# A causal mask read as 3 KB runs on 128 partitions, with a shuffle matrix in the band matmul, in a batched matmul and softmax

## Chip, cores, metric

One core of one Trainium2 chip. The metric is the device time of one execution in microseconds (us). A run is compared with runs of the kernel before on the same chip in the same job.

## The reference

```python
# x: 16 x 512 x 512, weight: 512 x 512, mask: 512 x 512 (1 strictly below the diagonal)
y = scale * np.matmul(x, weight)          # scale = 0.125
y = np.where(mask == 1, y, -1e9)
y_exp = np.exp(y - np.max(y, axis=-1, keepdims=True))
return (y_exp / np.sum(y_exp, axis=-1, keepdims=True)).astype(np.float32)
```

Row 0 is fully masked, so it comes out as 1/512 everywhere. Traffic that no version avoids is x (16.8 MB in) and the result (16.8 MB out).

## The kernel before

Work goes in 16 units u of 512 rows. Two units are a group of 2 MB: half h of the rows of four batches. For h = 0 only the left 256 columns are computed. A partition holds eight consecutive rows (slots t). One unit is: a cast of x to bf16 on VectorE (DVE), 16 transposes on TensorE (PE) into PSUM (PE's result memory), two copies back (DVE and ScalarE, called ACT), and then for each of the four slots four matmuls with the weight, one matmul that adds the mask's band (the 256 columns of this half in which the diagonal lies), the exponential on ACT with its row sum, and the division on DVE.

```python
load(0, slots(0))                       # first half of x group 0, 1 MB
for b in range(KT):                     # four diagonal 128x128 blocks of the mask
    seq(nc.sync.dma_start(diag_f32[b * DP : (b + 1) * DP],
        mask[r : r + P, r : r + P].rearrange("(p t) c -> p t c", t=S)))
seq(nc.sync.dma_start(w_f32, ...))      # weight, 1 MB
load(0, slots(1))
for g in range(1, X_BUFS): load(g)      # groups 1 to 4 of x, 2 MB each
...
spin(12)                                # filler matmuls on zeros: PE busy until data comes
...
cast(0); transpose(0); evict(0)
# diag_f32 -> 0 / -512 -> four matmuls that repeat rows -> eight copies -> band
...
for u in range(U + 1):
    if u + 1 < U: transpose(u + 1)
    if u + 2 < U: cast(u + 2)
    if u + 1 < U: evict(u + 1)
    if u < U:     multiply(u)
    if u >= 1:    normalise(u - 1); ...store, and load of group g + 5
```

Every transfer is issued by the SyncE queue (SP), in program order. Each is split over the same 16 DMA engines.

The softmax here doesn't subtract the row's maximum and nothing guards it: scores larger than these inputs give would overflow.

## Time and profile before

| | before |
|---|---|
| median time | 90.65 us (90.54 to 90.81) |
| span of the profiled run | 89.0 us |
| PE busy | 81% |
| DMA engines, data | 94% of 16 engines' span |
| moved | 34.95 MB |
| last store issued / last landing / end | 82.43 / 88.21 / 89.04 us |

Read it in this order: which resources are busy throughout, then which of them has work waiting in front of it. The prediction below does this with the lines. One part of the page that it doesn't show is that of the DMA issues (what, issuer, count, KB each, us from issue to landing):

```profile
xf<-in_x_dram SPq DMA_DIRECT2D x7, 2048.0 KB, 17.0
out_dram<-ot SPq DMA_DIRECT2D x6, 2048.0 KB, 13.8
diag_f<-in_mask_dram SPq DMA_DIRECT2D x4, 64.0 KB, 4.9
```

A transfer of 2 MB needs 4.9 us of engine time (the prediction's steps between landings) and lands 13.8 to 17 us after its issue: most of that it waits behind other transfers, so the DMA queue has work in front of it.

### The profile page before, as it was taken

The numbers are of one execution on the slowest core, as the hardware profiler recorded it, in microseconds if no ns is written. First come the engines' busy times: TensorE is split into PE (matmuls) and PEld (weight loads), VectorE is DVE, ScalarE is ACT, GpSimd is POOL, SyncE is SP. The second block draws the span as 40 slices with busy tenths as digits, with TensorE's granted clock in tenths as the row PEclk, the third lists the DMA queues.
The fourth block names the chain that finished last, engine by engine and source line by source line (L and its number), as shares of the span: only waits on it lengthen the run. The fifth ranks groups of instructions, "written<-read, shape, count | busy, mean of one in ns | idle before, by whom it ended". The sixth has DMA issues, their size and how long they took to land.

```text
span 89.0 us, 1583 instructions
## 1 busy us (share of the span) xinstructions
PE 72.1 (81%) x585; PEld 49.6 (56%) x592; DVE 61.0 (68%) x121; ACT 55.9 (63%) x154; POOL 6.6 (7%) x14
## 2 busy tenths in 40 slices
PE   4994503999999999999999999999999999980000
PEld 1324103878955659995565999556599965530000
DVE  4856785079994877999687699977689880528000
ACT  5300593445977868698687779768777977671000
POOL 7940000000200000020000002000000200000000
PEclk9999855558999999999999999999999999999555
DMA  0998999999999999999998999999999999999770
GB/s 11 390 228 328 420 464 434 405 449 420 427 434 405 434 394 427 467 427 375 456 442 383 471 427 383 464 434 397 449 427 405 449 420 420 456 401 420 324 320 15
DMA packets 3462, 34.95 MB, mean 392 GB/s; under 512 B 384, under 2 KB 896, under 8 KB 896
## 3 DMA queue, kind: packets, MB, share of 16 engines
q1 hardware_dynamic: 3456, 34.87, 94.0%
q8 instruction: 4, 0.07, 0.3%
q14 instruction: 2, 0.02, 0.0%
HBM read 18.09 MB, written 16.78 MB: 392 GB/s over the span
## 4 chain that ended last, share of the span: by engine, by line
PE 73%; DMA 10%; SPq 4%; DVE 3%; issue 1%; ACT 1%; DVEq 0%; ACTq 0%
PE py L122 48%; PE pt L98 16%; DMA xf<-in_x_dram 10%; PE py L131 8%; SPq L174 3%; DVE ot L158 1%; DVE xb L89 1%; SPq L85 1%; ACT ot L141 1%; SPq L179 1%; DVEq L290 0%; DVE rinv L156 0%; ACTq L290 0%
## 5 line engine op out<-in xcount | busy, mean ns | idle before, releaser
L122 PE MATMUL py<-w_bf,xt 128*128 128x256 bf16 (+1 forms) x249 | 51.0, 334 | 0.4
L141 ACT ACTIVATE ot<-py 128x256 f32<-128x256 f32 (+1 forms) x64 | 31.2, 493 | 8.9 <-PE py L131 8.8
L122 PEld LDWEIGHTS <-xt 128*128 128x128 bf16 x256 | 25.3, 101 | 12.8
L109 ACT COPY xt<-pt 128x1024 bf16<-128x1024 bf16 x16 | 16.2, 1012 | 12.8 <-PE pt L98 8.0
L89 DVE CAST xb<-xf 128x2048 bf16<-128x2048 f32 x16 | 19.5, 1221 | 5.8 <-DMA xf<-in_x_dram 5.8
L158 DVE TENSOR_SCALAR ot<-ot,rinv 128x256 f32<-128x256 f32 (+1 forms) x64 | 23.0, 423 | 0.7
L98 PE MATMUL pt<-ident_bf,xb 128*128 128x128 bf16 x256 | 17.8, 225 | 5.1 <-DVE xb L89 5.1
L98 PEld LDWEIGHTS <-xb 128*128 128x128 bf16 x256 | 16.6, 116 | 7.5 <-DVE xb L89 6.7
L131 PE MATMUL py<-band,ident_bf 128*128 128x256 bf16 x64 | 17.9, 280 | 0.0
L108 DVE COPY xt<-pt 128x1024 bf16<-128x1024 bf16 x16 | 11.0, 688 | 7.8 <-PE pt L98 7.8
L141 ACT ACTIVATION_READ_ACCUMULATOR ot<-py 128x1 f32 x64 | 12.8, 201 | 0.0
L131 PEld LDWEIGHTS <-ident_bf 128*128 128x128 bf16 x64 | 6.5, 101 | 4.3
L160 POOL MEMSET ot<- 4x256 f32 x4 | 1.8, 448 | 63.1 <-DVE ot L158 63.1
L190 PE MATMUL py<-zeros 128*128 128x512 bf16 x12 | 5.3, 632 | 1.2 <-DVE zeros L185 1.2
L156 DVE RECIPROCAL rinv<-rsum 128x4 f32<-128x4 f32 x16 | 2.7, 168 | 5.1 <-ACT ot L141 5.1
L198 DVE MEMSET ot<- 128x2048 f32 x2 | 3.5, 1765 | 0.8 <-issue 0.8
L190 PEld LDWEIGHTS <-zeros 128*128 128x128 bf16 x12 | 1.6, 144 | 3.9 <-issue 2.8
L233 ACT CAST band<-py 64x512 bf16<-64x512 f32 x4 | 2.3, 580 | 1.1 <-DVE band L233 1.0
L233 DVE CAST band<-py 64x512 bf16<-64x512 f32 x4 | 2.5, 675 | 0.5 <-PE py L222 0.5
L222 PE MATMUL py<-diag_bf,spread 64*128 64x512 bf16 x4 | 1.2, 412 | 0.9 <-DVE diag_bf L209 0.9
L196 POOL MEMSET band<- 64x2048 bf16 x1 | 1.8, 1800 | 0.1
L195 POOL MEMSET band<- 64x2048 bf16 x1 | 1.8, 1802 | 0.0
(14 smaller groups left out, 6.6 us busy)
## 6 DMA issues: line engine op xcount, KB each, us to landing
xf<-in_x_dram SPq DMA_DIRECT2D x7, 2048.0 KB, 17.0
out_dram<-ot SPq DMA_DIRECT2D x6, 2048.0 KB, 13.8
out_dram<-ot SPq DMA_DIRECT2D x4, 1024.0 KB, 9.6
xf<-in_x_dram SPq DMA_DIRECT2D x2, 1024.0 KB, 7.2
w_f<-in_weight_dram SPq DMA_DIRECT2D x1, 1024.0 KB, 6.9
diag_f<-in_mask_dram SPq DMA_DIRECT2D x4, 64.0 KB, 4.9
```

What stands on the lines that cost most here:

```text
L89: seq(nc.vector.tensor_copy(xb, st_x[u // 2][:, slots(u)]))
L98: nc.tensor.transpose(st_pt[u][kt // 2][:, kt % 2, t], xb[:, t].rearrange("p (k kt) -> p kt k", kt=KT)[:, kt], ident_bf,)
L108: seq(nc.vector.tensor_copy(xt[:, 0:2], pt[0]))
L109: seq(nc.scalar.copy(xt[:, 2:4], pt[1]))
L122: nc.tensor.matmul(py[:, :NC], lhsT=xt[:, kt, t], rhs=w_bf[:, kt, :NC], start=(kt == 0), stop=(kt == KT - 1),)
L131: nc.tensor.matmul(py[:, h * HB : NC], lhsT=ident_bf, rhs=band[:, h, slots(u)][:, t], start=False, stop=True, skip_group_check=True,)
L141: nc.scalar.activation(out=ot[:, t, :NC], in_=py[:, :NC], func=AF.Exp, bias=0.0, scale=float(scale), accum_out=rsum[:, t : t + 1],)
L156: seq(nc.vector.reciprocal(rinv, st_sum.pop(u)))
L158: seq(nc.vector.tensor_scalar_mul(ot[:, t, :NC], ot[:, t, :NC], rinv[:, t : t + 1]))
L190: seq(nc.tensor.matmul(idle, lhsT=zeros[:, :P], rhs=zeros, start=True, stop=True))
L198: nc.vector.memset(ots[i][:, :, HB:], 0.0)
L233: copy(band[half, h, slots(j), g * P : (g + 1) * P], pm.rearrange("p (t c) -> p t c", t=T)[half],)
```

## The change

Its intent: replace the mask's small blocks, and the matmuls and copies that spread them, by one transfer in which each partition p holds, for each half h, the run of 768 numbers that covers the bands of rows 2p and 2p+1. The band matmul, which had an identity matrix as its stationary operand, gets a shuffle matrix that picks the right rows. Beside that, the weight is issued ahead of the mask, twelve more filler matmuls stand after the first transposes, and the first two units multiply ahead of the next transposes.

```diff
-                    lhsT=ident_bf,
-                    rhs=band[:, h, slots(u)][:, t],
+                    lhsT=spread[:, (slots(u).start + t) // 2],
+                    rhs=band[:, h, t % 2],
 ...
     load(0, slots(0))
-    (four transfers of a 128x128 diagonal block)
     seq(nc.sync.dma_start(w_f32, ...))
+    RUN = N + HB
+    seq(nc.sync.dma_start(mask_f32, bass.AP(tensor=mask.tensor, offset=mask.offset,
+            ap=[[2 * N, P], [HB * (N + 1), 2], [1, RUN]])))
 ...
     cast(0)
     transpose(0)
+    spin(12)
     evict(0)
-    (conversion of diag, four matmuls, eight copies into band)
     (weight cast)
+    for i in range(2): band[:, :, i] = (mask_f32[:, :, i * N : i * N + HB] * 512 - 512)   # abridged
     cast(1)
     for u in range(U + 1):
+        if u < 2:
+            multiply(u)
         if u + 1 < U:
             transpose(u + 1)
         if u + 2 < U:
             cast(u + 2)
         if u + 1 < U:
             evict(u + 1)
-        if u < U:
+        if 2 <= u < U:
             multiply(u)
```

More of the change, by code (lines that the diff above doesn't have):

```diff
@@ L67 @@
     w_bf = const.tile([P, KT, N], BF16, name="w_bf")
-    diag_f32 = const.tile([HP, S, P], FP32, name="diag_f32")
-    diag_bf = const.tile([HP, S, P], BF16, name="diag_bf")
-    spread = const.tile([HP, 2, P], BF16, name="spread")
+    spread = const.tile([P, S // 2, P], BF16, name="spread")
     zeros = const.tile([P, N], BF16, name="zeros")
-    band = const.tile([P, 2, S, HB], BF16, name="band")
+    band = const.tile([P, 2, 2, HB], BF16, name="band")
     ots = [const.tile([P, S, N], FP32, name=f"ot{i}") for i in range(OUT_BUFS)]
@@ L168 @@
     load(0, slots(0))
-    DP = P // S
-    for b in range(KT):
-        r = b * P
-        seq(
-            nc.sync.dma_start(
-                diag_f32[b * DP : (b + 1) * DP],
-                mask[r : r + P, r : r + P].rearrange("(p t) c -> p t c", t=S),
-            )
+    seq(nc.sync.dma_start(w_f32, weight.rearrange("(p kt) n -> p kt n", kt=KT)))
+    RUN = N + HB
+    mask_f32 = ots[OUT_BUFS - 1].rearrange("p t n -> p (t n)")[:, : 2 * RUN].rearrange(
+        "p (h c) -> p h c", h=2
+    )
+    seq(
+        nc.sync.dma_start(
+            mask_f32,
+            bass.AP(
+                tensor=mask.tensor,
+                offset=mask.offset,
+                ap=[[2 * N, P], [HB * (N + 1), 2], [1, RUN]],
+            ),
         )
-    seq(nc.sync.dma_start(w_f32, weight.rearrange("(p kt) n -> p kt n", kt=KT)))
+    )
     load(0, slots(1))
@@ L194 @@
     make_identity(nc, ident_bf)
-    nc.gpsimd.memset(band[:HP, :, :, P:], MASK_NEG)
-    nc.gpsimd.memset(band[HP:, :, :, :P], 0.0)
     for i in range(0, OUT_BUFS, 2):
@@ L202 @@
     for e in range(E):
-        seq(nc.scalar.copy(spread.rearrange("k h (q e) -> k (h q) e", e=E)[:, :, e], ident_bf[:HP, :HP]))
+        seq(
+            nc.scalar.copy(
+                spread.rearrange("q j (p e) -> q j p e", e=E)[:, :, :, e],
+                ident_bf.rearrange("q (p j) -> q j p", j=S // 2),
+            )
+        )
     cast(0)
     transpose(0)
+    spin(12)
     evict(0)
-    seq(
-        nc.vector.tensor_scalar(
-            out=diag_bf,
-            in0=diag_f32,
-            scalar1=-MASK_NEG,
-            scalar2=MASK_NEG,
-            op0=ALU.mult,
-            op1=ALU.add,
-        )
-    )
-    for h in range(2):
-        for j in range(2):
-            pm = psum_y.tile([P, N], FP32, name="py")
-            seq(
-                nc.tensor.matmul(
-                    pm,
-                    lhsT=spread[:, h],
-                    rhs=diag_bf[:, slots(j)].rearrange("k t c -> k (t c)"),
-                    start=True,
-                    stop=True,
-                )
-            )
-            for g, copy in enumerate((nc.vector.tensor_copy, nc.scalar.copy)):
-                half = slice(g * HP, (g + 1) * HP)
-                seq(
-                    copy(
-                        band[half, h, slots(j), g * P : (g + 1) * P],
-                        pm.rearrange("p (t c) -> p t c", t=T)[half],
-                    )
-                )
     seq(nc.vector.tensor_copy(w_bf[:, 0:2], w_f32[:, 0:2]))
     seq(nc.scalar.copy(w_bf[:, 2:4], w_f32[:, 2:4]))
+    for i in range(2):
+        seq(
+            nc.vector.tensor_scalar(
+                out=band[:, :, i],
+                in0=mask_f32[:, :, i * N : i * N + HB],
+                scalar1=-MASK_NEG,
+                scalar2=MASK_NEG,
+                op0=ALU.mult,
+                op1=ALU.add,
+            )
+        )
     cast(1)
     for u in range(U + 1):
+        if u < 2:
+            multiply(u)
         if u + 1 < U:
```

## The prediction

> **What bounds the kernel now.** I read the forty slices first, then the table of stretches, then the DMA landings of the last stores, and the chain of waits last, because the chain misleads here. The slices of the kernel before:
>
> ```profile
> PE   4994503999999999999999999999999999980000
> PEclk9999855558999999999999999999999999999555
> DMA  0998999999999999999998999999999999999770
> GB/s 11 390 228 328 420 464 434 405 449 420 427 434 405 434 394 427 467 427 375 456 442 383 471 427 383 464 434 397 449 427 405 449 420 420 456 401 420 324 320 15
> DMA packets 3462, 34.95 MB, mean 392 GB/s; under 512 B 384, under 2 KB 896, under 8 KB 896
> ```
>
> One slice is 89.04/40 = 2.23 us. Two rows read 9 from slice 9 on, PE and DMA, and only one of them can be the bound. The stretches (columns: length, busy us of PE, PEld, DVE, ACT, POOL, clock, DMA share, GB/s):
>
> ```profile
> 6.50:14.50 8.00, 2.26 (x20) 1.30 (x20) 6.38 (x9) 4.38 (x6) 0.00 (x0) 0.74 0.99 402
> 14.50:21.00 6.50, 6.20 (x42) 5.03 (x43) 2.77 (x4) 2.56 (x8) 0.00 (x0) 0.53 0.99 421
> 21.00:79.80 58.80, 58.38 (x515) 41.60 (x519) 45.96 (x102) 46.21 (x135) 1.79 (x4) 1.00 1.01 427
> ```
>
> PE is busy 58.38 of 58.80 us in the long stretch and the DMA engines 1.01 of it. The way to decide is to ask which of the two has work lying in front of it. The chain of waits names PE:
>
> ```profile
> PE 73%; DMA 10%; SPq 4%; DVE 3%; issue 1%; ACT 1%; DVEq 0%; ACTq 0%
> ...
> 80.72 0.49 DVE ot L158
> 81.21 0.40 DVEq L290
> 81.61 0.79 DVE ot L158 x2
> ```
>
> It runs to the last multiply at 82.40 and the last store issue at 82.43, and leaves 6.6 us to the end. The DMA view of 82 to 83 us shows that last store:
>
> ```profile
> out_dram<-ot SPq DMA_DIRECT2D x1, 1024.0 KB, 5.8
> ```
>
> 1 MB at 427 GB/s is 2.46 us. The first issue of the run, at 0.74, has its first packet at 2.19 (trace), so 1.45 us of latency, and about 0.3 us goes to the last receipt: 4.2 us without a queue. It took 5.8, so about 1.6 us was spent behind other packets. The store before it (also 1 MB, issued 78.53) took 7.2 us. The landing records say more. One transfer counts up 16 times, once for each DMA engine. Last of the 16, in queue order: x 6.29, four mask blocks 6.72, 7.17, 7.60, 8.13, weight 11.01, second half of x group 0 13.50, group 1 18.38, ..., the last four stores 78.44, 83.30, 85.75, 88.21. The final steps of 2.45 us for 1 MB and 4.9 us for 2 MB are the pace of an engine that never waits (eight 8 KB packets of 0.309 us are 2.47). So on the slowest of the 16 engines the queue is full from the first packet to 88.21, though PE hands over its last result at 82.4. The fastest engines end the last store at 86.45: they do idle from about 82.9 to 84.0, waiting for PE (the 7s in slices 37 and 38). **The slowest DMA engine bounds the run; PE is about 1.9 us from taking over**, since that engine has the store before done at 85.75 and could start the last one at 82.43 + 1.45 = 83.9.
>
> **What the Trainium skill says.** "DMA: Bandwidth & Descriptors", Queues, rings and completion order: on each DMA engine descriptors are consumed in ring order and engines finish independently. The trace agrees: landings come strictly in order of issue, and the 16 counts of the last store spread over 86.45 to 88.21. The same page, Where 436 GB/s comes from, gives a ceiling of 435 GB/s; the trace holds 427 in the long stretch and 16 KB packets take 612 ns (26.8 GB/s an engine), so there is no spare rate. The same page, Why small descriptors are slow, has a fixed cost per packet: the median 512 B packet here took 27 ns (19 GB/s), the mean 39 ns. "TensorE: Matmul & The Clock Gate", What's actually happening, says that activity over windows of 3.4 us releases a halved clock. The trace agrees: 0.5 granted from 10.34 to 20.58, after the PE had stood idle for 4.02 us up to 14.80.
>
> **The change, part by part.** It does three things at the start and nothing in the steady part.
>
> Mask arithmetic. Removed: four matmuls with their eight evictions and the conversion, and two fills on POOL:
>
> ```profile
> L233 ACT CAST band<-py 64x512 bf16<-64x512 f32 x4 | 2.3, 580 | 1.1 <-DVE band L233 1.0
> L233 DVE CAST band<-py 64x512 bf16<-64x512 f32 x4 | 2.5, 675 | 0.5 <-PE py L222 0.5
> L222 PE MATMUL py<-diag_bf,spread 64*128 64x512 bf16 x4 | 1.2, 412 | 0.9 <-DVE diag_bf L209 0.9
> ```
>
> With the conversion (0.67 us, 1024 columns, in the timeline at 8.88) this is the DVE's work from 8.88 to 12.49. Added: two conversions of 512 columns, 2 x about 0.36 = 0.7 us (scaled from 0.67). DVE is free for the weight some 3 us sooner. The band matmul of the steady part changes its stationary matrix only: 64 x 128x256 as before, 0.11 us each on the path.
>
> PE order and clock. Twelve more filler matmuls after the first transposes (at full clock about 0.21 us each, half of the cold spacing of 0.43 in the timeline, so 2.6 us, from 8.7 to 11.3), and multiply(0) goes ahead of transpose(1). At a full clock a unit's transposes are 0.89 us instead of 1.90 and its four narrow products 0.55 instead of 1.07 each. Weight landed about 8.8 and mask about 10.8 (below) put multiply(0) at 11.3 to 13.6. Transpose(1) follows the cast of x at about 14.8 and multiply(1) ends about 18.8. Then transpose(2) waits for group 1 of x (18.1) and its cast (1.23), so from 19.6, and multiply(2) starts about 21.8 where it started at 24.8. **PE gains 3 us**, so its last store would be issued near 79.4. Two landings lie just ahead of it: group 7 of x (63.8; transposes that used it ran at 68.0) and the store that frees the fourth output buffer (68.7; first written at about 72.5). Both allow 3 us, not much more.
>
> Transfers. Mask bytes go from 4 x 64 KB = 262,144 to 256 runs of 3 KB = 786,432. Per engine: before, 32 packets of 512 B, on the slowest engine 8.13 - 6.29 = 1.84 us, then the weight 2.88 us (2.49 would be its own packets; first ones took up to 0.85 us) and x 2.49. After: weight 2.49, mask 16 packets of 3,072 B at 26.8 GB/s = 0.115, say 0.12 us each = 1.92, x 2.49. From 6.29 the second half of x lands at 13.19 in place of 13.50: **0.3 us less**. A check by bytes: 0.524 MB more at 427 GB/s is +1.23 us; the holes in slices 2 and 3 (228 and 328 instead of 427) are 2.23 x 298/427 = 1.55 us; the difference is again 0.3. The slow engine stood 0.65 us behind the next one when x landed (13.50 against 12.85); part of that may come from the small packets and go with them. I add 0.2 for it.
>
> Everything behind is the same queue in the same order, with the same bytes. The sum is -0.3 - 0.2 = -0.5 us, and the 3 us of PE are not in it: they become a longer queue in front of the last store.
>
> **The rivals.**
> - PE is the bound, as the chain says. Then 3 us earlier on PE is 3 us earlier at the end: 87.6 us, faster by over 3%. For it speak the chain and the idle time of the fast engines before the last store; against it 88.21 - 85.75 = 2.46, the slowest engine's back-to-back pace at the end.
> - The tripled mask costs more than the holes it closes, because 3 KB runs at a row pitch read worse than 8 KB ones: +1.2 us and no hole recovered, 91.8 us. For it: first packets after a change of transfer took 0.7 to 0.85 us. Against: after that 8 KB packets fall to 0.309.
> - The clock falls anyway (PE idles near 13.6 to 14.8 and 18.8 to 19.6) and PE gains little. The end would hardly move, because of the 1.9 us in hand.
> - The lag of the slow engine, 1.17 us to the fastest at 13.50, vanishes. Then the next one, 0.6 us ahead, bounds: about 89.7.
>
> **Range and chances.** Time runs 1.6 us above the span (90.65 against 89.0), so 90.65 - 0.5 = 90.15, say 90.2. The low end takes the vanished lag in full and 0.3 more, 89.4; the high end a mask that reads 0.7 us worse than worked out, 90.9. Faster by over 2% means under 88.84, which needs the PE rival: 0.06. Slower means over 92.46: 0.02. Same 0.92.
>
> **What would show it.** Right: the second half of x lands near 13.2, the long stretch stays at about 427 GB/s, PE ends near 77, the last store is issued near 79.5 and takes about 8.2 us instead of 5.8, slices 37 and 38 read 9, and the last landing is within 1 us of 88.2. Clock at 1.0 past slice 4. Wrong: the last store still takes under 6 us although it is issued 3 us earlier; or a steady rate well above 427; or mask packets well over 0.15 us each.

## The result, and the profile after

The changed kernel took 91.91 us (median of 4 runs, 91.8 to 91.99), the kernel before 90.73 (4 runs). The ratio is 1.013 (95% interval 1.0104 to 1.0155): slower by 1.3%, within the band called "same", and outside the predicted range of 89.4 to 90.9.

The slices of the changed kernel (PE busy, granted clock, DMA busy, rate; 2.25 us each), and its packets:

```profile
PE   4988974019999999999999999999999999990000
PEclk9999999855699999999999999999999999999955
DMA  1998999999999999998999999999999999999680
GB/s 22 331 430 361 411 426 466 430 386 466 437 415 415 349 382 430 455 459 371 430 459 415 422 430 415 422 444 437 408 437 430 422 437 422 437 422 411 266 346 11
DMA packets 3158, 35.47 MB, mean 394 GB/s; under 512 B 336, under 2 KB 336, under 8 KB 592
```

Three things to see. The early holes in the DMA rate are smaller, as intended (430 and 361 where before had 228 and 328). PE has a new hole in slices 7 and 8, followed by a halved clock in slices 8 to 10 (slices count from 0). And slice 13 has 349 GB/s with DMA at 9: busy engines that move less. The stretches of the changed kernel (length, busy us of PE, PEld, DVE, ACT, POOL, clock, DMA share, GB/s; a packet is counted where it starts, so a share can come out a little above 1):

```profile
6.50:14.50 8.00, 6.13 (x51) 4.11 (x52) 3.71 (x6) 3.85 (x10) 0.00 (x0) 1.00 0.99 412
14.50:21.00 6.50, 2.00 (x22) 1.53 (x21) 2.95 (x3) 1.01 (x1) 0.00 (x0) 0.70 1.01 434
21.00:26.00 5.00, 5.00 (x49) 4.08 (x48) 1.18 (x5) 2.67 (x9) 0.00 (x0) 0.70 1.00 423
26.00:81.00 55.00, 54.98 (x473) 37.98 (x470) 44.30 (x98) 43.50 (x124) 1.79 (x4) 1.00 1.00 423
```

From 6.5 to 14.5 PE does far more than before (6.13 us busy, clock 1.00, against 2.26 and 0.74). From 14.5 to 21 it has only 2.00 us to do, and the lead is gone. Its timeline on DVE and PE shows why:

```profile
13.06 1.23 DVE L87 CAST xb<-xf 128x2048 bf16<-128x2048 f32 x1 [1.73 <-DMA xf<-in_x_dram]
18.05 1.23 DVE L87 CAST xb<-xf 128x2048 bf16<-128x2048 f32 x1 [3.76 <-DMA xf<-in_x_dram]
19.19 0.68 DVE L106 COPY xt<-pt 128x1024 bf16<-128x1024 bf16 x1
...
14.35 1.09 PE L96 MATMUL pt<-ident_bf,xb 128*128 128x128 bf16 x16 [1.39 <-DVE xb L87]
19.93 0.82 PE L120 MATMUL py<-w_bf,xt 128*128 128x256 bf16 x3 [4.50 <-DVE xt L106]
```

Unit 1's transposes are done at 15.4. Their copy out of PSUM (L106) stands behind the cast of unit 2 on DVE, and that cast waits for group 1 of x until 18.05. So PE waits 4.50 us, its clock falls, and the first wide product starts at 25.87 instead of 24.65 (timeline). The last store is issued later than before, at 83.65 instead of 82.43:

```profile
out_dram<-ot SPq DMA_DIRECT2D x1, 1024.0 KB, 5.3
```

The steady part is as it was. Two groups of the changed kernel's page (line, operation, count, busy us, mean ns):

```profile
L129 PE MATMUL py<-band,spread 128*128 128x256 bf16 x64 | 17.9, 280 | 0.0
L220 DVE TENSOR_SCALAR band<-ot 128x512 bf16<-128x512 f32 x2 | 0.8, 424 | 1.6 <-DMA ot<-in_mask_dram 1.6
```

The band matmul with the shuffle matrix takes the 280 ns that it took with the identity, and the two conversions that replace the old mask work take 0.42 us each, against 0.36 expected.

Now the landings, from the trace's records of each engine's count (us; "9th" is the ninth of the 16 counts, "last" the sixteenth; the counts do not name their engine, so "the ninth engine" below is the middle of the pack and not always the same one):

| transfer | before 9th | before last | after 9th | after last |
|---|---|---|---|---|
| x group 0, first half | 5.66 | 6.29 | 5.56 | 5.67 |
| mask complete | 7.48 | 8.13 | 10.30 | 10.54 |
| weight | 9.98 | 11.01 | 8.04 | 8.22 |
| x group 0, second half | 12.46 | 13.50 | 12.77 | 13.04 |
| x group 2 | 22.25 | 23.28 | 22.57 | 22.82 |
| x group 3 | 27.14 | 28.74 | 27.45 | 29.21 |
| x group 4 | 32.04 | 33.62 | 32.86 | 35.07 |
| store of group 6 | 81.05 | 83.30 | 81.86 | 84.09 |
| last store but one | 83.47 | 85.75 | 84.31 | 86.63 |
| last store | 86.63 | 88.21 | 87.80 | 88.99 |

The last count goes from 86.63 to 88.99 in 2.36 us, and the trace has eight packets of 0.309 us back to back from 86.20 to 88.65 before it: in the changed kernel, too, the engine that ends last does not wait for PE, though PE is late. So the 0.78 us at the end must be found inside the DMA queue, and the table has two steps of about that sum. By the second half of x the ninth engine is 0.31 later. In the load of group 4 it loses another 0.51: this load takes 5.41 us instead of 4.90. The stretches that this load and the one before it fill, of the kernel before:

```profile
22.20:27.10 4.90, 4.85 (x44) 3.54 (x44) 4.86 (x12) 4.15 (x13) 0.45 (x1) 1.00 1.02 428
27.10:32.00 4.90, 4.90 (x38) 2.88 (x37) 3.28 (x8) 3.80 (x10) 0.00 (x0) 1.00 0.99 420
```

and of the changed kernel:

```profile
22.60:27.40 4.80, 4.80 (x49) 3.53 (x48) 2.57 (x7) 3.28 (x9) 0.45 (x1) 0.86 1.02 430
27.40:32.80 5.40, 5.40 (x41) 3.16 (x39) 5.33 (x13) 4.02 (x11) 0.00 (x0) 1.00 0.97 375
```

At a DMA share of 0.97 the rate is 375 instead of 420 GB/s: some 16 KB packets take 0.7 to 1.5 us there in place of 0.612 (trace, 28.8 to 31.5 us). I call this the slow stretch.

### The profile page after: what moved, and what is told of

The parts are those of the page before. It is cut to its first block, busy times and chain, and to the rows that moved or that the text cites. A ratio compares the mean times of both kernels' runs of the same rounds, so it can differ in the third digit from the quotient of the medians.

```text
span 90.0 us, 1595 instructions
## 1 busy us (share of the span) xinstructions
PE 73.4 (82%) x600; PEld 49.4 (55%) x600; DVE 58.6 (65%) x118; ACT 54.3 (60%) x150; POOL 3.1 (3%) x12
## 4 chain that ended last, share of the span: by engine, by line
PE 68%; DMA 16%; DVE 3%; SPq 2%; issue 2%; ACT 1%; DVEq 0%; ACTq 0%
PE py L120 46%; DMA xf<-in_x_dram 16%; PE pt L96 14%; PE py L129 8%; DVE ot L156 1%; SPq L83 1%; DVE xt L106 1%; ACT ot L139 1%; SPq L167 1%; SPq L175 0%; DVEq L282 0%; DVE rinv L154 0%; ACTq L282 0%; DVE xb L87 0%; DVEq L87 0%
## 5 line engine op out<-in xcount | busy, mean ns | idle before, releaser
L96 PE MATMUL pt<-ident_bf,xb 128*128 128x128 bf16 x256 | 16.8, 219 | 1.9 <-DVE xb L87 1.9
L96 PEld LDWEIGHTS <-xb 128*128 128x128 bf16 x256 | 15.8, 114 | 3.9 <-DVE xb L87 3.1
L129 PE MATMUL py<-band,spread 128*128 128x256 bf16 x64 | 17.9, 280 | 0.0
L106 DVE COPY xt<-pt 128x1024 bf16<-128x1024 bf16 x16 | 11.0, 687 | 9.8 <-PE pt L96 6.0
L139 ACT ACTIVATION_READ_ACCUMULATOR ot<-py 128x1 f32 x64 | 12.8, 199 | 0.0
L194 PE MATMUL py<-zeros 128*128 128x512 bf16 x24 | 8.1, 505 | 1.2 <-DVE zeros L189 1.2
L129 PEld LDWEIGHTS <-spread 128*128 128x128 bf16 x64 | 6.5, 101 | 4.3
L194 PEld LDWEIGHTS <-zeros 128*128 128x128 bf16 x24 | 2.8, 122 | 5.1 <-issue 2.7
L220 DVE TENSOR_SCALAR band<-ot 128x512 bf16<-128x512 f32 x2 | 0.8, 424 | 1.6 <-DMA ot<-in_mask_dram 1.6
L206 ACT COPY spread<-ident_bf 128x128 bf16<-128x128 bf16 x4 | 1.3, 522 | 0.0
L217 ACT CAST w_bf<-w_f 128x1024 bf16<-128x1024 f32 x1 | 1.0, 1048 | 0.0
```

The lines of the kernel that those rows point to most:

```text
L96: nc.tensor.transpose(st_pt[u][kt // 2][:, kt % 2, t], xb[:, t].rearrange("p (k kt) -> p kt k", kt=KT)[:, kt], ident_bf,)
L106: seq(nc.vector.tensor_copy(xt[:, 0:2], pt[0]))
L129: nc.tensor.matmul(py[:, h * HB : NC], lhsT=spread[:, (slots(u).start + t) // 2], rhs=band[:, h, t % 2], start=False, stop=True, skip_grou ...
L139: nc.scalar.activation(out=ot[:, t, :NC], in_=py[:, :NC], func=AF.Exp, bias=0.0, scale=float(scale), accum_out=rsum[:, t : t + 1],)
L194: seq(nc.tensor.matmul(idle, lhsT=zeros[:, :P], rhs=zeros, start=True, stop=True))
L206: nc.scalar.copy(spread.rearrange("q j (p e) -> q j p e", e=E)[:, :, :, e], ident_bf.rearrange("q (p j) -> q j p", j=S // 2),)
```

## The experiments

Theory A: PE, delayed by the order on DVE, sets the end. Theory B: the DMA engines set it, and the loss is made of a dearer mask and the slow stretch. Eighteen kernels ran, the later ones to find the cause of the stretch. This table has all of them, with the ninth engine's landing of x's second half, the length of the load of the fifth x transfer (ninth count to ninth count) and the last landing, from the one profiled run of each (it was the slowest of the kernel's runs in e12, e13 and e14 and the fastest in the changed kernel, e7 to e11, e15 and e18, so times are compared by the ratio and not by the last landing):

| kernel | median us | before, same job | ratio (95% interval) | second half lands | fifth load | last landing |
|---|---|---|---|---|---|---|
| before | | | | 12.46 | 4.90 | 88.21 |
| changed | 91.91 | 90.73 | 1.0130 (1.0104 to 1.0155) | 12.77 | 5.41 | 88.99 |
| e1 | 92.11 | 91.03 | 1.0122 (1.0078 to 1.0165) | 12.73 | 5.45 | 89.07 |
| e2 | 90.82 | 91.03 | 0.9987 (0.9963 to 1.0010) | 12.52 | 4.90 | 88.16 |
| e3 | 91.06 | 91.03 | 1.0024 (0.9972 to 1.0075) | 12.52 | 4.92 | 88.45 |
| e4 | 91.77 | 91.03 | 1.0101 (1.0062 to 1.0140) | 12.78 | 5.34 | 89.08 |
| e5 | 90.53 | 91.00 | 0.9951 (0.9914 to 0.9988) | 10.48 | 6.21 | 87.76 |
| e6 | 90.98 | 91.00 | 0.9994 (0.9962 to 1.0026) | 12.73 | 4.89 | 88.50 |
| e7 | 91.20 | 91.00 | 1.0028 (0.9989 to 1.0067) | 13.14 | 4.89 | 88.32 |
| e8 | 92.28 | 91.00 | 1.0154 (1.0111 to 1.0196) | 14.05 | 4.89 | 89.17 |
| e9 | 91.64 | 90.68 | 1.0107 (1.0059 to 1.0155) | 12.78 | 5.40 | 88.59 |
| e10 | 90.38 | 90.68 | 0.9946 (0.9910 to 0.9982) | 10.57 | 5.98 | 87.38 |
| e11 | 92.16 | 90.68 | 1.0144 (1.0105 to 1.0183) | 12.74 | 5.31 | 88.86 |
| e12 | 90.34 | 90.68 | 0.9957 (0.9915 to 0.9998) | 11.17 | 5.52 | 88.07 |
| e13 | 92.07 | 91.10 | 1.0094 (1.0053 to 1.0134) | 13.52 | 4.90 | 89.49 |
| e14 | 91.45 | 91.10 | 1.0024 (0.9978 to 1.0069) | 13.23 | 4.93 | 89.22 |
| e15 | 92.00 | 90.84 | 1.0121 (1.0081 to 1.0162) | 12.73 | 5.35 | 88.95 |
| e16 | 90.42, one run | 91.10 | | 10.63 | 6.11 | 87.80 |
| e17 | 91.88, one run | 91.10 | | 12.81 | 5.27 | 89.06 |
| e18 | 90.34 | 90.84 | 0.9935 (0.9905 to 0.9966) | 10.63 | 5.83 | 87.38 |

### Does PE set the end? (e1, e4, e2)

e1 takes the wait out of DVE's way:

```diff
+        if u < 1:
+            evict(u + 1)
         if u + 2 < U:
             cast(u + 2)
-        if u + 1 < U:
+        if 1 <= u and u + 1 < U:
             evict(u + 1)
```

> The changed kernel with one swap: on VectorE the copy of the second unit's transposes out of PSUM goes ahead of the cast that waits for group 1 of x. Theory A (the DVE queue made PE late, and PE sets the end): PE's idle time of 4.5 us at 15.4 to 19.9 falls below 1.5, the first wide product starts near 21.5 to 22.5 instead of 25.9, the last store is issued near 80.5 instead of 83.65, and the time falls by 1.2 us or more, to 90.7 or less. Theory B (the DMA engines set the end: more mask bytes on every engine, and a slow stretch of packets at 29 to 31 us): the same on PE, but the last landing stays within 0.4 us of 89.0 and the time between 91.5 and 92.2.

On DVE the copy now runs at once, in e1's timeline, and PE follows:

```profile
13.12 1.23 DVE L87 CAST xb<-xf 128x2048 bf16<-128x2048 f32 x1 [1.96 <-DMA xf<-in_x_dram]
15.30 0.69 DVE L106 COPY xt<-pt 128x1024 bf16<-128x1024 bf16 x1 [0.96 <-PE pt L96]
18.05 2.36 DVE L87 CAST xb<-xf 128x2048 bf16<-128x2048 f32 x2 [2.05 <-DMA xf<-in_x_dram]
...
16.05 0.39 PE L120 MATMUL py<-w_bf,xt 128*128 128x256 bf16 x2 [0.34 <-DVE xt L106]
21.39 0.81 PE L120 MATMUL py<-w_bf,xt 128*128 128x512 bf16 x2
```

The first wide product starts at 21.39 instead of 25.87 and the last store is issued at 81.18 instead of 83.65. The time does not move (1.0122 against 1.0130), and the last store simply stands 7.9 us in the queue:

```profile
out_dram<-ot SPq DMA_DIRECT2D x1, 1024.0 KB, 7.9
```

So PE's lost lead is real, and worth nothing here.

e4 keeps the new mask but runs the first two units in the old order:

```diff
-        if u < 2:
-            multiply(u)
 ...
-        if 2 <= u < U:
+        if u < U:
             multiply(u)
```

> The changed kernel with its mask and its filler matmuls, but the first two units in the old order (transpose ahead of the products). Theory A: the products of the first unit fill the time in which the cast waits, the first wide product starts near 23.5, and the time falls by 1 us or more against the changed kernel, to 90.9 or less. Theory B: PE is 2 us earlier and the time stays within 0.4 us of 91.9.

The last store is issued at 81.19, and the ratio is 1.0101, with an interval that overlaps those of e1 and of the changed kernel. Theory B again.

e2 asks the same of the kernel before, by taking work from PE (the result is wrong):

```diff
-            seq(nc.tensor.matmul(py[:, h * HB : NC], lhsT=ident_bf,
-                    rhs=band[:, h, slots(u)][:, t], start=False, stop=True, ...))
```

> The kernel before without the 64 band matmuls (7 us of PE's path, about 4 of them before the last group; the result is wrong on purpose). If the slowest DMA engine bounds the kernel before, as the prediction says, the time moves by less than 0.7 us (90.0 to 90.9), and the last store waits longer between issue and landing (10 us or more in place of 5.8). If PE bounds it, the time falls to 87 or less.

The ratio is 0.9987. In the stretches of e2, PE is now idle for 4 of 56.5 us while DMA stays full:

```profile
21.00:77.50 56.50, 52.56 (x439) 35.45 (x440) 45.18 (x101) 44.87 (x133) 1.79 (x4) 0.97 1.01 428
```

The last store is issued at 80.00 and takes 8.2 us. It was expected to take 10 or more, because I took all of PE's saving for lead; PE meets the DMA landings first. The kernel before is bound by its DMA engines, and the prediction's rival that PE is the bound has fallen.

### What the mask transfer costs (e3, e5, e6, e7, e8)

e3 adds to e1 a mask transfer of the bands alone, in 1 KB packets:

```diff
     (abridged)
-            ap=[[2 * N, P], [HB * (N + 1), 2], [1, RUN]]           # one transfer, 786 KB
+    for h in range(2):                                             # two of 262 KB
+            offset=mask.offset + h * HB * (N + 1), ap=[[2 * N, P], [N, 2], [1, HB]]
```

> As e1, and the mask comes as two transfers of the bands alone: per engine 32 packets of 1 KB (524 KB in all) in place of 16 of 3 KB (786 KB). Theory B: each engine is 0.4 us sooner with the mask (1 KB at 26.8 GB/s is 0.038 us and some 0.006 for the packet), so the time is 0.3 to 0.5 us under e1's. Theory A: the mask bytes lie beside PE's work and the time equals e1's within 0.15 us.

The second half of x lands at 12.52, 0.21 sooner than in e1, and the fifth load takes 4.92. Its stretch in e3:

```profile
27.20:32.10 4.90, 4.85 (x43) 3.35 (x42) 4.87 (x9) 3.80 (x10) 0.00 (x0) 1.00 0.99 411
```

The ratio falls from 1.0122 to 1.0024 in the same job, about 0.9 us: more than expected of either theory, because the slow stretch went as well. With e1 this shows that the mask transfer's form, not the order of work, made the changed kernel slower. It does not tell fewer bytes from shorter packets, since e3 has both.

e5 is e1 with no mask transfer (the tile is filled with ones on the chip; wrong):

```diff
-    seq(nc.sync.dma_start(mask_f32, bass.AP(...)))
+    nc.gpsimd.memset(mask_f32, 1.0)
```

> As e1 (copy ahead of the waiting cast), with no mask transfer at all: the mask tile is filled with ones on the chip, so the result is wrong on purpose. The mask's 16 packets of 3 KB take 2.25 us of each engine (half of x group 0 at 12.77 less weight at 8.04 less 2.47). If the DMA engines set the end, every landing is 2.2 us sooner and the time falls by 2.2 us or more against e1, to 89.9 or less; with the slow stretch near 30 us gone as well, by 2.7. If something of PE's path is left in it, by under 1.5 us.

The second half of x lands 2.25 us sooner, as worked out, but the fifth load takes 6.21 us where e1's takes 5.45, so 0.76 us is given back. Against the kernel before, the ratio is 0.9951 where e1's is 1.0122: some 1.6 us, where 2.2 or more was expected of a DMA bound and under 1.5 if PE's path had a share. In the stretches of e5 the load of group 4 has

```profile
25.20:31.40 6.20, 6.15 (x56) 4.54 (x56) 6.13 (x13) 5.08 (x16) 0.00 (x0) 1.00 0.98 322
```

so the slow stretch needs neither 3 KB packets nor a mask. That was a surprise, and it rules out that only long mask packets bring it about.

e6 is the kernel before with the weight ahead of the mask blocks:

```diff
     load(0, slots(0))
+    seq(nc.sync.dma_start(w_f32, ...))
     (four mask blocks)
-    seq(nc.sync.dma_start(w_f32, ...))
```

> The kernel before with one change: the weight is issued ahead of the four mask blocks, so that no engine runs out of packets behind the short ones. Theory B: the hole at 6.0 to 6.9 us goes, 32 packets of 27 ns make 0.9 us for the mask, the half of x group 0 lands at 11.6 in the middle engine instead of 12.46, and the time falls by 0.7 to 1.0 us against the kernel before, to 89.7 to 90.1. Theory A: PE starts at the cast of that half all the same, 0.8 sooner, and so a fall of about the same size, but with a last store that waits no longer than 5.8 us; under theory B it waits about as long, too, since both move; so this run is for its use, not to tell A from B.

A miss: 0.9994. The four blocks take as long as before (ninth count 8.31 to 10.25, 1.94 us, where 32 packets of 27 ns would be 0.9), so the second half of x lands no sooner (12.73). So the hole behind the short packets was not the cost. The four transfers take their 1.9 us wherever they stand, with gaps between packets whose median is 27 ns.

e7 adds 128 KB of useless reading to the kernel before, to shift the queue:

```diff
+    seq(nc.sync.dma_start(ots[OUT_BUFS - 1]...[:, :HB], weight.rearrange(...)[:, :HB]))
```

> The kernel before with one more transfer of 128 KB behind the weight (8 packets of 1 KB per engine, to a place nobody reads). It puts the queue 0.3 to 0.4 us back, as the tripled mask does, without 3 KB runs. Is the slow stretch of packets at 29 to 31 us a matter of the queue's position in time, it shows here too, and the time rises by 0.8 us or more; is it a matter of the 3 KB runs, it does not, and the time rises by 0.3 to 0.4.

The ninth engine is 0.68 later at the second half of x, no slow stretch follows (4.89), and the time rises by 0.28%, 0.25 us, with an interval that includes no change. Inconclusive on 3 KB runs, since e5 had shown the stretch without any.

e8 adds 256 KB to e3, in packets of 2 KB, so that the bytes are those of the changed kernel:

> As e3 (bands alone, 1 KB packets) with one more transfer of 256 KB (8 packets of 2 KB per engine), so that the bytes are those of the changed kernel. If bytes alone make the loss, the time is that of e1 (1.2 per cent over the kernel before); if the slow stretch near 30 us needs the 3 KB runs, the time is 0.4 to 0.5 us under e1's and the fifth load of x takes 4.9 us, not 5.4.

```diff
+    seq(nc.sync.dma_start(ots[OUT_BUFS - 1]...[:, 4 * HB : 6 * HB], weight.rearrange(...)[:, : 2 * HB]))
```

It can't be read as planned: that extra read alone took 2.04 us on the ninth engine (9.48 to 11.52), three times what its bytes need at 427 GB/s. The queue is 1.6 us late, there is no slow stretch, and the time is 1.0154. It does show that a loss of this size in the queue alone, without a slow stretch, comes out at the end.

### What decides the slow stretch (e9 to e18)

The first theory was the time of issue. e9, e10 and e11 hold back the load of group 4 until the first cast is done, without changing its place in the queue (added to e1, to e5 and to the changed kernel):

```diff
-    for g in range(1, X_BUFS):
+    for g in range(1, X_BUFS - 1):
         load(g)
 ...
     cast(0)
+    st_x[X_BUFS - 1] = x_pool.tile([P, S, K], FP32, name="xf")
+    seq(nc.vector.memset(st_x[X_BUFS - 1][:, 0, :1], 0.0))
+    load(X_BUFS - 1)
```

> As e1, but the load of x group 4 is issued after the first cast, near 7 us, in place of 5.2 (a one-column fill of its buffer makes it wait). Nothing changes its place in the queue, which it reaches at 27.3 us. In the eight kernels so far the slow stretch within this load went with its time of issue: 1.3 us of stretch where it was issued at 4.7, 0.4 to 0.6 at 5.2, 0.1 at 6.2, none from 7.6 on. Theory C (an early issue of this load causes the stretch): the load takes 4.9 us in place of 5.4 and the time falls by 0.4 to 0.6 against e1. Theory D (the stretch comes from the place of the load in the queue or in time): no change, within 0.2 us of e1.

> As e5 (no mask transfer, wrong on purpose) with the same hold of the load of x group 4 until near 7 us. Theory C: the 6.1 us of that load become 4.9, and the time falls by 1.0 to 1.3 us against e5, to 89.2 to 89.5; then the mask transfer is worth its full 2.2 us at the end. Theory D: the time stays at 90.5 within 0.2.

> The changed kernel itself with the hold alone, its order of work as it is. Theory C: 0.4 to 0.6 us less than the changed kernel, so 0.7 to 0.9 over the kernel before or a ratio of 1.006 to 1.010; what remains is the larger mask. If it stays at 1.013, the hold does nothing.

It was issued at 7.14, 7.33 and 6.98 us, and took 5.40, 5.98 and 5.31 us. Theory C has fallen; the correlation behind it was an accident of the first eight kernels.

e12 loads one mask block in place of four in the kernel before (wrong):

```diff
-    for b in range(KT):
+    nc.vector.memset(diag_f32, 0.0)
+    for b in range(1):
```

> The kernel before with one mask block loaded in place of four (wrong on purpose), so that eight transfers stand ahead of the first store, none waits, and the load of x group 4 is issued near 5.3 us in place of 7.8. Theory C: the slow stretch appears here too, the load takes 5.3 us or more instead of 4.9. With 1.0 us less of mask on every engine and 0.5 lost in the stretch the time falls by 0.3 to 0.7. Theory D: the load keeps its 4.9 us and the time falls by 1.0 us.

The stretch appears (5.52 us) and the ratio is 0.9957, some 0.4 us. The number met Theory C, but e9 to e11, in the same job, rule its reason out. What e12 leaves: the kernel before has the stretch, too, when its queue is 1.3 us ahead. It needs nothing of the change.

The next four kernels changed what stands ahead of the load. e13 is e1 with the mask in two transfers of 384 columns; e14 adds three transfers of 16 x 64 bytes to e1; e16 adds four such to e5; e17 loads group 4 ahead of group 3 in e1:

```diff
+    for i in range(2): ...mask_f32[:, :, i * HR : (i + 1) * HR]... ap=[[2 * N, P], [HB * (N + 1), 2], [1, HR]]   # e13
+    for i in range(3): seq(nc.sync.dma_start(ots[OUT_BUFS - 1][:16, 7, 16 * i : 16 * i + 16], weight[:16, :16]))  # e14; 4 in e16
-    for g in range(1, X_BUFS):
+    for g in (1, 2, 4, 3):                                                                                         # e17
```

> As e1, with the mask in two transfers of 384 columns of each run, so 32 packets of 1.5 KB per engine in place of 16 of 3 KB: same bytes, 8 transfers and 88 descriptors ahead of the load of group 4 instead of 7 and 71. If the count of transfers or of descriptors ahead decides, the load takes 4.9 us instead of 5.4 and the time falls by 0.3 to 0.5 us against e1 (to 1.006 to 1.009 of the kernel before). If the bytes decide, nothing changes.

> As e1, with three more transfers of 16 rows of 64 bytes (one descriptor and one count per engine each): 10 transfers and 77 descriptors ahead of the load of group 4. If the count of transfers decides (the 9th and later ones wait for the counter of an earlier one), the slow stretch goes, and the load takes 4.9 us; if the count of descriptors decides, it stays at 5.3 to 5.5.

> As e5 (no mask transfer, wrong on purpose) with four such small transfers: 10 transfers and 62 descriptors ahead of the load of group 4. The same question where the stretch is longest: 4.9 us for the load if transfers decide (and a time near 89.4), 6.0 or so if descriptors do (and 90.5).

> As e1 with group 4 of x loaded ahead of group 3. If the stretch belongs to the rows of group 4, it moves with them to the fourth place, at 24 to 27 us; if to the fifth load or to the time of 29 to 31 us, it stays there and meets group 3. PE waits longer for group 3, which says nothing here.

e13 has no stretch, but its 1.5 KB packets made the mask take 3.07 us instead of 2.26, and the time stays at 1.0094. e14 has next to none on the ninth engine (4.93), and a ratio of 1.0024 although its queue is half a microsecond later than e1's. e16, with as many transfers ahead as e14, keeps the stretch (6.11), so the number of transfers doesn't decide. e17 keeps it in the fifth place, where it now meets group 3:

```profile
22.60:27.50 4.90, 4.86 (x38) 2.73 (x36) 3.18 (x8) 3.56 (x10) 0.00 (x0) 1.00 1.00 428
27.50:32.80 5.30, 5.25 (x46) 3.71 (x45) 3.37 (x7) 4.20 (x13) 0.00 (x0) 1.00 1.00 390
```

so it is not a matter of which rows of x are read.

e15 and e18 put the weight in 2 KB runs, which changes the number of descriptors and their size, not the bytes (e15 from e1, e18 from e5):

```diff
-    w_f32 = const.tile([P, KT, N], FP32, name="w_f32")
+    w_f32 = const.tile([P, KT, N + 16], FP32, name="w_f32")[:, :, :N]
```

> As e1, with the weight in 2 KB runs (its rows in the tile padded by 64 bytes): 95 descriptors ahead of the fifth load of x in place of 71, same bytes, same transfers. If the number of descriptors decides, that load takes 4.9 us instead of 5.4 and the time is 0.3 to 0.5 us under e1 less some 0.15 for the shorter runs. If it only happened to go along, the load keeps 5.3 to 5.5 us.

> As e5 (no mask transfer, wrong on purpose), with the weight in 2 KB runs: 78 descriptors ahead in place of 54. If the number decides, the load falls from 6.2 us to 5.2 or less and the time by about 1 us, to 89.4 to 89.7. If not, it stays at 6.0 or more and the time at 90.3 to 90.6; then what decides stays open.

The load took 5.35 and 5.83 us. The number of descriptors went along with the stretch and doesn't decide it. **What triggers the stretch stays open.** What the runs leave standing: it lies in the fifth x load, at 27 to 32 us; it is longest where the queue is earliest (6.0 us on average for the four kernels whose second half landed at 10.5 to 10.6), 5.3 to 5.5 for eight kernels at 11.2 to 12.8, and absent or nearly so in the four at 13.1 or later. But before, e2, e3 and e6, whose masks came in packets of 1 KB or less, were at 12.46 to 12.73 and had none, so earliness alone is not it either.

No correct version beat the kernel before: the nearest ones, e6, e3, e14 and e7, are its equals.

## Why the prediction was wrong

**What bounds the kernel: right.** "The slowest DMA engine bounds the run" is shown by e2 (PE relieved, 0.9987) and by e1 and e4 (PE's last store 2.5 us sooner, same time). That PE was near taking over is right as well: in the changed kernel the fast engines idle before the last store, as slices 37 and 38 show.

**"PE gains 3 us": wrong, and harmless.** The step had transpose(1) followed by multiply(1) ending at 18.8, and so gave unit 1's copy a free DVE. The order of DVE's program, which was there to be read, has cast(2) ahead of it, and cast(2) waits for x until 18.05. PE lost 1.22 us to the kernel before (25.87 against 24.65) instead of gaining 3. e1 restored the gain to 3.3 us (21.39), and the end did not follow. The clock, said to hold past slice 4, fell at 17.15 for the same reason. The prediction had misread the clock in the kernel before, too: 0.5 was granted from 10.34, ahead of the idle time of 10.78 to 14.80 behind which it puts it. PE was busy for 1.82 of the 3.41 us up to 10.34.

**"0.3 us less" on the transfers: the step that failed first.** The sum was made on the engine that was last at 13.50 us, whose mask and weight had 0.4 us of extra waiting in them. On that last count the forecast came true, 13.04 in place of 13.50, but partly by luck: the mask took 2.32 us there (8.22 to 10.54) instead of 1.92, and the first half of x happened to land at 5.67 instead of 6.29. The gain did not reach the end, because something else decides who is last from group 3 of x on. At 24.3 us (23.6 in the changed kernel) one 16 KB instruction fetch holds an engine: fetch and the data packet behind it take 1.1 us each where a data packet alone takes 0.612, and by group 3 of x one engine is 1.7 to 1.9 us behind the first, in both kernels (28.74 against 27.01; 29.21 against 27.36). In the changed kernel the last count at group 2 was just 0.36 behind the first, so the new last one came out of the ordinary pack. For an ordinary engine the sum reads (ninth counts): before, mask 7.48 - 5.66 = 1.82, weight 2.50, x 2.48; after, weight 2.48, mask 10.30 - 8.04 = 2.26, x 2.47. The mask term was worked out as 16 x 0.12 = 1.92 and measured 2.26. The packets did take 0.121 us, but with gaps between them; the term that it replaces was 1.82, not 1.84 + 0.4. Net +0.41, less 0.10 by which the first half of x landed sooner: +0.31 in place of -0.31. The 0.2 us added for the vanished lag was right as an observation (the lag at the second half of x fell from 1.04 to 0.27) and wrong as a gain, because another engine takes over the last place.

**The missing term: the slow stretch, 0.51 us.** "Everything behind is the same queue in the same order, with the same bytes" holds, but not the conclusion that it takes the same time: the fifth load ran at 375 instead of 420 GB/s. +0.31 and +0.51 make +0.82; the last landing moved by 88.99 - 88.21 = 0.78, and the span by 0.97, since 0.19 more passes after the last landing (the medians differ by 1.18). Both terms all but go in e3, which changes the mask's transfer alone against e1 and stands at 1.0024; so the loss comes with that transfer.

How much each term costs is bookkeeping on landings, not an experiment, and other runs warn against reading it one for one. Take the kernels timed in rounds whose second half of x landed at 12.5 to 13.2. The six with the stretch (changed, e1, e4, e9, e11, e15) stand at 1.010 to 1.014, the five without (e2, e3, e6, e7, e14) at 0.999 to 1.003. Yet e7 and e14 were 0.68 and 0.77 us later than the kernel before, more than the 0.31. In e7 the ninth engine is still 0.70 late at the store of group 6 (81.75 against 81.05), but the last one only 0.12 (83.42 against 83.30). So the loss goes with the stretch, and it is not shown that the 0.31 alone costs anything. e8 and e13, 1.59 and 1.06 later and without a stretch, do show a cost of a late queue.

**The rivals.** "PE is the bound" has fallen. "The tripled mask costs more than the holes it closes" was the right rival, with 91.8 us forecast and 91.91 measured, but not by its numbers: it had the queue 1.2 us later behind the mask, and it was 0.31, with a stretch beside it that nobody had foreseen. That the totals meet is luck. "The clock falls anyway, and the end hardly moves because of the time in hand" was right on the clock; PE went further and lost time, and the end moved, but not through PE. "The lag of the slow engine vanishes" came true at the second half of x and brought nothing at the end.

**The range.** Its upper end allowed 0.7 us for a mask that reads worse. It had nothing for a change in how later transfers run, while the chances held: the outcome is in the class that had 0.92.

## What to carry to other kernels

When all 16 DMA engines are full from start to end, work out a change's cost on an ordinary engine and not on the one that happens to be last early: who is last changes during the run. Then follow the last engine to the end, too: in e7 it did not move with the ordinary one. Fewer and longer packets do not pay by themselves if they carry three times the bytes; here 32 packets of 512 B cost each engine 1.82 to 1.94 us, 32 of 1 KB 2.02 and 16 of 3 KB 2.26. And read the order of every in-order engine ahead of a claim about a gain: a cast that waits for data holds up every copy behind it.

## What the Trainium skill lacked or had wrong

- "Runtime: NRT & Kernel Launch", Instruction fetch mechanics, calls the cost of crossing a 16 KiB boundary mostly hidden. For the sequencer that may be so; for a saturated DMA queue it is not: four fetches of 16 KB in each trace, the first at 18.8 to 25.8 us, and in the kernel before each takes 0.93 to 1.10 us and the data packet behind it 1.01 to 1.09, where a data packet alone takes 0.612; after the first, one engine is 1.7 us behind the first engine for the load in flight (28.74 against 27.01).
- "DMA: Bandwidth & Descriptors", Why small descriptors are slow, explains a fixed cost per packet. On the 2 KB row pitch of this mask the cost does not follow the packet's size: mask transfers per engine took 1.94 us for 32 packets of 512 B (e6), 2.02 for 32 of 1 KB (e3), 3.07 for 32 of 1.5 KB (e13) and 2.26 for 16 of 3 KB. The 3 KB figure runs from 2.07 to 2.34 over the eight kernels with that transfer. No section gives figures for such patterns at a row pitch as small as this.
- The same page has nothing like the slow stretch: a plain 2 MB load with full engines at 375 GB/s where the one before it runs at 430, in the changed kernel (322 against 435 in e5), and a load of 5.27 us or more in 12 of the 20 kernels, with 16 KB packets up to 1.5 us long in the changed one. The runs don't settle its cause either.
- "TensorE: Matmul & The Clock Gate", What's actually happening, has the clock fall after an idle window of about 3.4 us. Here it fell after a window with PE 1.82 of 3.41 us busy (6.93 to 10.34 us in the kernel before) and did not rise after one with 2.37 busy (13.76 to 17.17), while in e2 it rose after one with 2.91 busy (13.84 to 17.25). So a window need not be idle for the clock to fall, and the page has no number for how busy it must be.
